# Writing a head's scaled context keys as two halves straight from their bank, with the norm's place and one step changed

## The chip, the core and the metric

The kernel runs on one core of a Trainium2 chip. The metric is the device time of one execution in microseconds (us); the lower the better. The engines are named as in the profile: PE is TensorE (PEld its weight loads), DVE is VectorE, ACT is ScalarE, POOL is GpSimd, and SP issues most transfers.

## The reference

One layer of a block over 256 latent tokens with 256 context tokens, model width 2048, batch 1, float32. Cut to what matters here:

```python
u = layer_norm(x) * (1 + scale) + shift          # and u_c from the context
p, p_c = u @ w_in, u_c @ w_in[:, :N_KV]          # one projection, split by columns
st_f = mlstm_final_state(kc, vc, *gf_c)          # context: C = sum_t w_t k_t v_t
h_f, _ = mlstm_chunked(ql, kl, vl, *gf_l, st_f)  # latent, forward and backward
h_l = h_f + flip(h_b)                            # 8 heads, keys 128, values 256
o_attn = attend_blocks(q_l, k_all, v_all)        # 16 query heads, 4 key heads
h = rms_norm(h_l per head, mh_norm_w)
y_a = (sigmoid(o_a) * h * silu(z_a)) @ w_ba
y_b = (o_attn * silu(z_b)) @ w_bb
out = (sigmoid(g_a) * y_a + sigmoid(g_b) * y_b) @ w_out
x_new = layer_norm(ALPHA * x + gate * out)
```

The change is in the eight heads of the first branch: the state `C` of a head is a product of the context's values with its keys, each key scaled by a weight `w_t` of its token and direction.

## The kernel before

**Products in three.** Every float32 operand of a product is split in two: ACT rounds it to a high half (`nc.scalar.copy`, L337) and DVE subtracts that from the original to get the low half (L338). `three` and `three_b` (L340 and on) make each product of three matmuls: high x high, high x low, low x high. So a weight block (`raw`, 128x1024, one transfer of SP) gets a cast by ACT (`whi`) and a subtraction by DVE (`wlo`) before PE can use it. Three buffers of each rotate, and `LEAD` asks for two blocks to be split ahead.

**Heads inside the gemms.** The gemms stream the weights: two for each `c` in 0 to 3, with the output gate's weights (`o`) and the silu gate's (`z`), of 32 ticks each, a tick being three matmuls of 512 columns (a triple). `head(h)` is a generator whose pieces are the steps of a head; `weave` spreads the steps over the ticks of a gemm. Head 0 lies in the `z` gemm of `c` = 0, head 1 in the next `o` gemm, and so on; head 7 lies in the first gemm of the second branch (`q`). Even heads lie in `z` gemms, odd heads in `o` gemms.

**A head's steps**, each ended by a `yield`: (1) fetch the rows of decays into `ws` through the POOL queue, transpose the context keys into a bank `pk` on PE (L849), scale them by the weights `G["wc"]` into `kw` by four ACT writes (L853), split `kw` into the halves `kwh` and `kwl` of the tile `rd`, split the context values into `rd` too; (2) split the latent keys and queries into `rc` (`kqh`, `kql`); (3) nothing; (4) and (5) the states of the two directions, `pC`, from `kwh`, `kwl` and the values, each split into `ra`; (6) `ws` becomes the decay matrix (L878 to L882, with an exponential on ACT) and the scaled queries (`rb`); (7) the scores `pS`, multiplied into `ws`; (8) `ws` split, its low half into `rc`, and the latent values into `ra`; (9) nothing; (10 to 13) four products `ph`, by tokens and direction, with a small division on DVE (L919 to L921) and the sum into `hh`; (14) the norm's root, on DVE and POOL (`rr`); (15) the norm applied to `hh`, two DVE instructions (L934); (16) transposes `pT` and their split.

**Two heads overlap.** Steps 14, 15 and 16 of a head are taken out of its list and put into the next head's list at places 1, 7 and 10:

```python
    for h in range(8):
        st = steps(head(h), HEAD_STEPS)
        if h > 0:
            for at, step in zip((1, 7, 10), order[-3:]):
                st.insert(at, step)
            order = order[:-3]
        order += st
```

**What sets the order.** The written order gives each instruction a priority; a scheduler then places instructions on the engines by its own estimate of their times. On each engine they run strictly in the order so found, and each waits for what it needs. PE's products stand as they are written; DVE and ACT are where the scheduler moves things. Banks: eight hold 512 float32 a partition each, four under the name `acc` for the gemms and four under `aux`, which `pk`, `pC`, `pS`, `pT` and `ph` take in turn.

Of the kernel before, what the change touches and what calls it, by code (L numbers as in the profile page):

```python
# [8 lines left out]
F32 = mybir.dt.float32  # L9
F32R = mybir.dt.float32r  # L10
BF16 = mybir.dt.bfloat16
AF = mybir.ActivationFunctionType
ALU = mybir.AluOpType
AX = mybir.AxisListType

P = 128
# [34 lines left out]
def block_kernel(ctx: ExitStack, tc: tile.TileContext, a: dict, out: bass.AP):  # L51
    nc = tc.nc
# [12 lines left out]
    def nm(s):  # L65
        uid[0] += 1
        return f"{s}_{uid[0]}"

    def slot(n, dt=F32):
        return big.tile([P, BIG], dt, tag="S8", name=nm(n))  # L70
# [7 lines left out]
    def t2(n):  # L78
        return tp.tile([P, 512], F32, tag="T2", name=nm(n), bufs=4)


    def sm(n, w):
        return tp.tile([P, w], F32, tag=f"sm{w}", name=nm(n), bufs=SMALL[w])
# [4 lines left out]
    def aux(n):  # L88
        return ps.tile([P, 512], F32, tag="aux", name=nm(n))
# [14 lines left out]
    def halves(x):  # L104

        return x.rearrange("p (n w) -> p w n", w=2)

    def as_halves(x):
        return x.rearrange("p (w n) -> p w n", w=2)
# [210 lines left out]
    def split_ahead(k):  # L320
        while len(ready) < k and (plan or early):
            fetch_ahead()
            raw, n = early.pop(0)
            turn[0] += 1
            pool, k_ = (late[0], 1) if late and turn[0] % 3 == 0 else (wp, 2)
            lo = pool.tile([P, 1024], F32R, tag="wlo", name=nm("wlo"), bufs=k_)[:, :n]
            hi = pool.tile([P, 1024], F32R, tag="whi", name=nm("whi"), bufs=k_)[:, :n]
            split(hi, lo, raw)
            ready.append((hi, lo))
# [5 lines left out]
    def split(hi, lo, src):  # L335

        nc.scalar.copy(hi, src)  # L337
        nc.vector.tensor_tensor(lo, src, hi.bitcast(F32), op=ALU.subtract)  # L338

    def three(o, xh, xl, wh, wl, start, stop):  # L340
        mm(o, lhsT=xh, rhs=wh, start=start, stop=False)  # L341
# [36 lines left out]
    def steps(gen, n):  # L378

        return [lambda: next(gen, None) for _ in range(n)]  # L380
# [158 lines left out]
    end, j = 0.0, 0  # L539
    for i, (c, k0, k1) in enumerate(VISITS):  # L540
        end += (k1 - k0) * (1.8 if chunks[c][1] == "w_kv" else 2.65)
        j0, j = j, max(j, min(len(units), math.ceil((end - T0) * 6 / DT)))
# [19 lines left out]
    G = {}  # L562
# [107 lines left out]
    def conv(x, hd, n, scale):  # L670

        ac = t2("cva")[:, :n * 256].rearrange("p (s t) -> p s t", s=n)
        sg = t2("cvs")[:, :n * 256].rearrange("p (s t) -> p s t", s=n)
        nc.scalar.activation(ac, x[:, :, 1:257], AF.Identity, bias=cv[:, hd, 3:4], scale=cv[:, hd, 1:2])
        nc.vector.scalar_tensor_tensor(ac, x[:, :, 0:256], cv[:, hd, 0:1], ac, op0=ALU.mult, op1=ALU.add)
        nc.vector.scalar_tensor_tensor(ac, x[:, :, 2:258], cv[:, hd, 2:3], ac, op0=ALU.mult, op1=ALU.add)
        nc.scalar.activation(sg, ac, AF.Sigmoid)
        nc.vector.scalar_tensor_tensor(x[:, :, 1:257], ac, scale, sg, op0=ALU.mult, op1=ALU.mult)
# [75 lines left out]
    j = 32  # L754
# [35 lines left out]
    gate_of = [None] * 4  # L790
# [35 lines left out]
        held.extend(lambda t=t: put_z(t) for t in range(2))  # L826
        gate_of[c] = g_

    HEAD_STEPS = 16

    def head(h):
        c, j = h // 2, h % 2
        kx = kT[h // 4][:, h % 4]
        kl = kx[:, 0, 1:257]
        q = qT[:, h, 1:257]
        stt = nc.vector.scalar_tensor_tensor
# [7 lines left out]
        kwh, kwl = (rd[:, i * 512:(i + 1) * 512] for i in range(2))  # L844
        vch, vcl = (rd[:, 1024 + i * 516:1024 + (i + 1) * 516].rearrange("p (t f) -> p t f", t=2)
                    for i in range(2))
        pk = aux("pk")
        for t in range(2):
            nc.tensor.transpose(pk[:, t * P:(t + 1) * P], kx[:, 1, 1 + t * P:1 + (t + 1) * P], ident)  # L849
        kw = t2("kw")  # L850
        for d in range(2):
            for t in range(2):
                nc.scalar.activation(kw[:, (2 * d + t) * P:(2 * d + t + 1) * P], pk[:, t * P:(t + 1) * P],  # L853
                                     AF.Identity, bias=0.0, scale=G["wc"][:, d, t, h:h + 1])
        split(kwh, kwl, kw)
        split_v(vch, vcl, va[c][:, 2:4, j, :])
        yield

        rc = wslot("rc", F32R)
        wl, kqh, kql = rc[:, 0:768], rc[:, 768:1280], rc[:, 1280:1792]  # L860
        split(kqh[:, 0:256], kql[:, 0:256], kl)
        split(as_halves(kqh[:, 256:512]), as_halves(kql[:, 256:512]), halves(q))
        yield
        yield

# [3 lines left out]
        for d in range(2):  # L869
            pc = aux("pC")  # L870
            for t in range(2):
                sl = slice((2 * d + t) * P, (2 * d + t + 1) * P)
# [17 lines left out]
        for t in range(2):  # L890
            sl = slice(t * P, (t + 1) * P)
# [8 lines left out]
        split_v(vh, vl, va[c][:, 0:2, j, :])  # L900
        yield
        yield

        hh = t2("hh").rearrange("p (t d) -> p t d", t=2)
        intra = {(0, 0): [(0, 0)], (0, 1): [(128, 0), (640, 1)],
# [2 lines left out]
        for t in range(2):  # L908
            for d in range(2):
                ph = aux("ph")  # L910
                sl = slice(d * 256 + t * P, d * 256 + (t + 1) * P)
# [18 lines left out]
        rr = sm("rr", 2)  # L930
        rsqrt(rr, ss, 1.0 / 256.0, EPS)
        yield
        for t in range(2):
            stt(hh[:, t, :], hh[:, t, :], rr[:, t:t + 1], gate_of[c][:, t, j * 256:(j + 1) * 256],  # L934
                op0=ALU.mult, op1=ALU.mult)
        yield
        pT = aux("pT")
        for f in range(2):
# [5 lines left out]
    def split_v(hi, lo, src):  # L944

        by = lambda x: x.rearrange("p t (w n) -> p t w n", w=2)
        split(by(hi), by(lo), src.rearrange("p t (n w) -> p t w n", w=2))
# [21 lines left out]
# [7 lines that stand above are left out]
    n = HEAD_STEPS  # L976
    order = [lambda h=h: conv(qT[:, h:h + 1, :], h, 1, 1.0) for h in range(8)] + order
# [183 lines left out]
    for k4 in range(4):  # L1161
        hi, lo = slot("wh", F32R), slot("wl", F32R)
        for b in range(2):
            raw = wp.tile([P, 1024], F32, tag="raw", name=nm("raw"), bufs=3)
            nc.sync.dma_start(raw, a["w_out"][3][2 * k4 + b])
            sl = slice(b * 1024, (b + 1) * 1024)
            split(hi[:, sl], lo[:, sl], raw)
        wl.append((hi, lo))
    for t in range(2):
        pp = acc("out")  # L1170
        for k in range(KT):
            sl = slice((k % 4) * 512, (k % 4 + 1) * 512)
# [99 lines left out]
```

## Time and profile before

| | |
|---|---|
| time, median of 3 runs | 1344.13 us (1340.24 to 1344.71) |
| the profiled execution | 1343.62 us, span 1341.6 us, 2.0 us around it |
| mean granted clock of PE | 0.991 |
| busy in the span | PE 97%, DVE 73%, ACT 48%, POOL 4% |
| the heads' stage | about 466 to 700 us of the span |

How to read it: PE is nearly always busy, so what a change of DVE or ACT work can give or take is the time in which PE waits for them. The wait rows name the line that waits and the line that let it go on; the rows of single instructions give their starts, so that a wait can be read as a start that comes late after the one before.

### The profile page before, as it was taken

Reading aid. Unit: us, or ns where it says so; the run is one execution under the profiler, and the core shown is the slowest. Engines: PE = TensorE matmul, PEld = TensorE weight load, DVE = VectorE, ACT = ScalarE, POOL = GpSimd, SP = SyncE. Lnnn points to the kernel's source line nnn. Section 1 sums busy time; section 2 is a strip of 40 time slices with the busy share of each in tenths; the row PEclk is TensorE's granted clock in tenths of the full one; section 3 lists DMA queues with packets and bytes.
Section 4 is the critical chain, followed back from the end, with each engine's and each line's share of the span. In section 5 each row is a group of like instructions: output and inputs, shape, how many; then the busy total and the mean of one; then the engine's idle time right before and its main releaser. Section 6 shows DMA issues by size and latency. Waiting matters only on the chain.

```text
span 1341.6 us, 19662 instructions
## 1 busy us (share of the span) xinstructions
PE 1296.4 (97%) x7541; PEld 1161.7 (87%) x7541; DVE 976.0 (73%) x1577; ACT 649.8 (48%) x928; POOL 54.1 (4%) x83
## 2 busy tenths in 40 slices
PE   6999998999999999999999999999999999999996
PEld 3788988999999988888889999998888888888884
DVE  6698998877986678787787868786555455545667
ACT  4544322324334576676755566565444444434441
POOL 0000000000110011010110000000000000000000
PEclk8999998999999999999999999999999999999999
DMA  9876764885435554555455444445655556576663
GB/s 339 310 260 227 251 221 136 296 306 189 143 111 189 195 167 160 171 181 180 155 162 182 139 161 142 143 139 174 204 198 202 204 197 203 195 275 219 218 219 116
DMA packets 77902, 264.17 MB, mean 197 GB/s; under 512 B 8984, under 2 KB 11688, under 8 KB 77168
## 3 DMA queue, kind: packets, MB, share of 16 engines
q1 hardware_dynamic: 74752, 251.99, 55.5%
q0 software_dynamic: 2448, 10.68, 2.4%
q8 instruction: 59, 0.97, 0.3%
q10 hardware_dynamic: 608, 0.24, 0.1%
q14 instruction: 35, 0.29, 0.1%
HBM read 260.75 MB, written 2.14 MB: 196 GB/s over the span
## 4 chain that ended last, share of the span: by engine, by line
PE 46%; DVE 2%; ACT 1%; DMA 1%; issue 0%; DVEq 0%; ACTq 0%
PE zb L347 2%; PE zb L346 2%; PE zb L348 2%; PE yb L343 2%; PE yb L342 2%; PE yb L341 2%; PE ga L343 2%; PE ga L341 2%; PE ga L342 2%; PE ya L343 2%; PE ya L341 2%; PE ya L342 2%; PE gb L342 2%; PE gb L343 2%; PE gb L341 2%; PE q L342 2%
## 5 line engine op out<-in xcount | busy, mean ns | idle before, releaser
L338 DVE TENSOR_TENSOR wlo<-raw,whi 128x1024 fp32r<-128x1024 f32 (+3 forms) x375 | 445.3, 1190 | 264.5 <-ACT whi L337 259.4
L337 ACT CAST whi<-raw 128x1024 fp32r<-128x1024 f32 (+3 forms) x375 | 380.2, 1016 | 449.2 <-PE p L343 130.8
L342 PE MATMUL p<-wlo,u 128*128 128x512 f32 (+1 forms) x448 | 160.1, 357 | 2.5 <-DVE wlo L338 2.4
L341 PE MATMUL p<-whi,u 128*128 128x512 f32 (+1 forms) x448 | 159.3, 358 | 2.1 <-ACT u L302 1.1
L225 DVE SCALAR_TENSOR_TENSOR junk<-mod,sc 128x1024 bf16<-128x1024 f32 x128 | 153.4, 1221 | 9.4 <-DMA mod<-in_w_mod 9.3
L343 PE MATMUL p<-whi,u 128*128 128x512 f32 (+1 forms) x448 | 159.4, 356 | 0.0
L342 PEld LDWEIGHTS p<-wlo,u 128*128 128x128 f32 x448 | 86.5, 193 | 10.8 <-DVE wlo L338 4.2
L341 PEld LDWEIGHTS p<-whi,u 128*128 128x128 f32 x448 | 85.7, 192 | 11.5 <-ACT u L302 2.5
L343 PEld LDWEIGHTS p<-whi,u 128*128 128x128 f32 x448 | 86.6, 193 | 6.8
L346 PE MATMUL zb<-u,whi 128*128 128x256 f32 x256 | 72.0, 281 | 0.0
L346 PE MATMUL p<-u,whi 128*128 128x256 f32 x256 | 70.6, 278 | 0.7 <-ACT u L302 0.7
L348 PE MATMUL p<-u,wlo 128*128 128x256 f32 x256 | 70.3, 275 | 0.2 <-DVE wlo L338 0.2
L347 PE MATMUL zb<-u,whi 128*128 128x256 f32 x256 | 70.4, 275 | 0.0
L348 PE MATMUL zb<-u,wlo 128*128 128x256 f32 x256 | 70.4, 275 | 0.0
L347 PE MATMUL p<-u,whi 128*128 128x256 f32 x256 | 70.4, 275 | 0.0
L346 PEld LDWEIGHTS p<-u,whi 128*128 128x128 f32 x256 | 48.9, 192 | 2.1 <-ACT u L302 1.2
L341 PE MATMUL z<-whi,u 128*128 128x512 f32 x128 | 49.7, 389 | 0.0
L341 PE MATMUL q<-whi,u 128*128 128x512 f32 x128 | 49.7, 388 | 0.0
L347 PEld LDWEIGHTS p<-u,whi 128*128 128x128 f32 x256 | 49.1, 192 | 0.4 <-issue 0.4
L342 PE MATMUL gb<-wlo,u 128*128 128x512 f32 x128 | 48.7, 381 | 0.8 <-DVE wlo L338 0.8
L342 PE MATMUL z<-wlo,u 128*128 128x512 f32 x128 | 49.2, 384 | 0.2 <-DVE wlo L338 0.2
L348 PEld LDWEIGHTS p<-u,wlo 128*128 128x128 f32 x256 | 49.1, 192 | 0.3 <-DVE wlo L338 0.3
(329 smaller groups left out, 3156.9 us busy)
## 6 DMA issues: line engine op xcount, KB each, us to landing
mod<-in_w_mod SPq DMA_DIRECT2D x96, 512.0 KB, 4.9
raw<-in_w_g SPq DMA_DIRECT2D x64, 512.0 KB, 4.1
raw<-in_w_o SPq DMA_DIRECT2D x32, 512.0 KB, 3.5
raw<-in_w_z SPq DMA_DIRECT2D x32, 512.0 KB, 3.6
raw<-in_w_qb SPq DMA_DIRECT2D x32, 512.0 KB, 3.6
raw<-in_w_zb SPq DMA_DIRECT2D x32, 512.0 KB, 3.4
raw<-in_w_ba SPq DMA_DIRECT2D x32, 512.0 KB, 3.5
raw<-in_w_bb SPq DMA_DIRECT2D x32, 512.0 KB, 4.1
```

Of the source, the lines that this page charges most:

```text
L225: nc.vector.scalar_tensor_tensor(junk, blk, 1.0, sc[v][:, hf * 1024:(hf + 1) * 1024], op0=ALU.mult, op1=ALU.mult, accum_out=mp[:, v, hf, j ...
L337: nc.scalar.copy(hi, src)
L338: nc.vector.tensor_tensor(lo, src, hi.bitcast(F32), op=ALU.subtract)
L341: mm(o, lhsT=xh, rhs=wh, start=start, stop=False)
L342: mm(o, lhsT=xh, rhs=wl, start=False, stop=False)
L343: mm(o, lhsT=xl, rhs=wh, start=False, stop=stop)
L346: mm(o, lhsT=wh, rhs=xh, start=start, stop=False)
L347: mm(o, lhsT=wh, rhs=xl, start=False, stop=False)
L348: mm(o, lhsT=wl, rhs=xh, start=False, stop=stop)
```

## The change

Three edits. The four scaled writes go from the bank `pk` straight into `kwh` (rounded to the high half as they are written), and each is followed by a DVE instruction that reads the same bank, multiplies by the same weight and subtracts the high half, into `kwl`; the tile `kw`, its cast and its single subtraction are gone. The two instructions that apply the norm get an order behind the low half of the next head's queries (`keys_done`). And a head has one more empty step, behind step 8, so that a gemm of 32 ticks carries 17 steps where it carried 16.

```diff
     def split(hi, lo, src):
 
         nc.scalar.copy(hi, src)
-        nc.vector.tensor_tensor(lo, src, hi.bitcast(F32), op=ALU.subtract)
+        return nc.vector.tensor_tensor(lo, src, hi.bitcast(F32), op=ALU.subtract)
...
-    HEAD_STEPS = 16
+    HEAD_STEPS = 17
+    keys_done = []
...
-        kw = t2("kw")
         for d in range(2):
             for t in range(2):
-                nc.scalar.activation(kw[:, (2 * d + t) * P:(2 * d + t + 1) * P], pk[:, t * P:(t + 1) * P],
-                                     AF.Identity, bias=0.0, scale=G["wc"][:, d, t, h:h + 1])
-        split(kwh, kwl, kw)
+                sl, wc = slice((2 * d + t) * P, (2 * d + t + 1) * P), G["wc"][:, d, t, h:h + 1]
+                src = pk[:, t * P:(t + 1) * P]
+                nc.scalar.activation(kwh[:, sl], src, AF.Identity, bias=0.0, scale=wc)
+                stt(kwl[:, sl], src, wc, kwh[:, sl].bitcast(F32), op0=ALU.mult, op1=ALU.subtract)
         split_v(vch, vcl, va[c][:, 2:4, j, :])
         yield
...
-        split(as_halves(kqh[:, 256:512]), as_halves(kql[:, 256:512]), halves(q))
+        keys_done.append(split(as_halves(kqh[:, 256:512]), as_halves(kql[:, 256:512]), halves(q)).ins)
...
         split(wh, wl, w)
         split_v(vh, vl, va[c][:, 0:2, j, :])
+        yield
         yield
         yield
...
-        for t in range(2):
-            stt(hh[:, t, :], hh[:, t, :], rr[:, t:t + 1], gate_of[c][:, t, j * 256:(j + 1) * 256],
-                op0=ALU.mult, op1=ALU.mult)
+        with tc.issue_after(keys_done[-1]):
+            for t in range(2):
+                stt(hh[:, t, :], hh[:, t, :], rr[:, t:t + 1],
+                    gate_of[c][:, t, j * 256:(j + 1) * 256], op0=ALU.mult, op1=ALU.mult)
```

The edits shift what the scheduler places around them. First DVE, from the low half of head 3's decays (`rc<-ws`) to the building of head 4's `ws`; before:

```order
L338 TENSOR_TENSOR rc_5591<-ws_5554,rb_5682 128x768
L338 TENSOR_TENSOR act_5738<-pT_5733,act_5738 128x512
L338 TENSOR_TENSOR wlo_5755<-raw_5696,whi_5756 128x1024
L919 SCALAR_TENSOR_TENSOR r_5768<-ph_5761,gT 128x1
L920 TENSOR_TENSOR r_5768<-ph_5761,r_5768 128x1
L921 RECIPROCAL r_5768<-r_5768 128x1
L338 TENSOR_TENSOR wlo_5804<-raw_5727,whi_5805 128x1024
L878 SCALAR_TENSOR_TENSOR ws_5846<-ws_5846,gT,cst 128x256
L879 SCALAR_TENSOR_TENSOR ws_5846<-ws_5846,gT,cst 128x256
L880 SCALAR_TENSOR_TENSOR ws_5846<-ws_5846,gT,cst 128x128
L919 SCALAR_TENSOR_TENSOR r_5789<-ph_5779,gT 128x1
L881 SCALAR_TENSOR_TENSOR ws_5846<-ws_5846,gT,cst 128x128
```

and in the changed kernel, whose lines stand one to three further down:

```order
L338 TENSOR_TENSOR rc_5595<-ws_5557,rb_5686 128x768
L338 TENSOR_TENSOR wlo_5759<-raw_5700,whi_5760 128x1024
L338 TENSOR_TENSOR act_5742<-pT_5737,act_5742 128x512
L879 SCALAR_TENSOR_TENSOR ws_5850<-ws_5850,gT,cst 128x256
L338 TENSOR_TENSOR wlo_5808<-raw_5731,whi_5809 128x1024
L921 SCALAR_TENSOR_TENSOR r_5775<-ph_5768,gT 128x1
L880 SCALAR_TENSOR_TENSOR ws_5850<-ws_5850,gT,cst 128x256
L922 TENSOR_TENSOR r_5775<-ph_5768,r_5775 128x1
L881 SCALAR_TENSOR_TENSOR ws_5850<-ws_5850,gT,cst 128x128
L923 RECIPROCAL r_5775<-r_5775 128x1
L882 SCALAR_TENSOR_TENSOR ws_5850<-ws_5850,gT,cst 128x128
```

The first of the four instructions on the fetched `ws` now stands ahead of a weight block's low half and of the first division, which both stood before it; the other three are mixed with the division.

Second DVE again, where head 4's context keys get their low halves (`rd<-kw` before, `rd<-pk` after) and head 3's norm is applied; before:

```order
L338 TENSOR_TENSOR rd_5848<-va_876,rd_5848 128x516
L128 TENSOR_SCALAR rs_5874<-ss_5760 128x2
L934 SCALAR_TENSOR_TENSOR hh_5759<-hh_5759,rr_5873,G_5025 128x256 x2
L338 TENSOR_TENSOR wlo_5895<-raw_5802,whi_5896 128x1024
L338 TENSOR_TENSOR rd_5848<-kw_5852,rd_5848 128x512
L338 TENSOR_TENSOR rc_5883<-kT_444,rc_5883 128x256
L338 TENSOR_TENSOR rc_5883<-qT_3947,rc_5883 128x256
```

and after:

```order
L856 SCALAR_TENSOR_TENSOR rd_5852<-pk_5853,gT,rd_5852 128x128
L923 RECIPROCAL r_5840<-r_5840 128x1
L338 TENSOR_TENSOR rc_5888<-kT_444,rc_5888 128x256
L927 SCALAR_TENSOR_TENSOR hh_5766<-ph_5833,r_5840,hh_5766 128x256
L856 SCALAR_TENSOR_TENSOR rd_5852<-pk_5853,gT,rd_5852 128x128
L338 TENSOR_TENSOR rc_5888<-qT_3947,rc_5888 128x256
L338 TENSOR_TENSOR wlo_5900<-raw_5806,whi_5901 128x1024
L856 SCALAR_TENSOR_TENSOR rd_5852<-pk_5853,gT,rd_5852 128x128
L128 TENSOR_SCALAR rs_5879<-ss_5767 128x2
L937 SCALAR_TENSOR_TENSOR hh_5766<-hh_5766,rr_5878,G_5027 128x256 x2
L856 SCALAR_TENSOR_TENSOR rd_5852<-pk_5853,gT,rd_5852 128x128
```

The norm stands behind the queries' low half (`rc<-qT`) now, but still ahead of the last of the four low halves. In odd heads the product of the silu gate (`sz`) stands at that place instead of the norm.

Third ACT, the same keys of head 4 in the changed kernel, with what each instruction waits for (an engine's name is its semaphore):

```order
L855 ACTIVATE rd_5852<-pk_5853,gT 128x128 [waits PE_49]
L337 CAST rc_5888<-kT_444 128x256
L337 CAST rc_5888<-qT_3947 128x256
L855 ACTIVATE rd_5852<-pk_5853,gT 128x128 [waits DVE_49]
L337 CAST whi_5901<-raw_5806 128x1024 [waits DMAHW4_49,PE_49,Activation_49]
L929 ACTIVATE sq_5845,ss_5767<-hh_5766 128x256 [waits DVE_49]
L855 ACTIVATE rd_5852<-pk_5853,gT 128x128 [waits DVE_49]
L812 ACT_TABLE_LOAD
L812 ACTIVATE G_5605<-o_5606 128x512 [waits PE_49]
L855 ACTIVATE rd_5852<-pk_5853,gT 128x128 [waits DVE_49]
```

Before, these four writes stood together, the second to fourth without a wait; now each waits for DVE's low half of the one before, and other work stands between them. On PE the order keeps nine triples between `pk` and the first `pC` (eight in head 7). The scores `pS` come one triple earlier, the first `ph` has nine triples behind `pS` where it had seven (seven for five in head 7), and one triple less lies between the last `ph` and the next `pk`.

## Rows read from the trace of the kernel before

**Rows 1.** The page's head and its first row: busy time, share, instructions.

```profile
span 1341.6 us, 19662 instructions
PE 1296.4 (97%) x7541; PEld 1161.7 (87%) x7541; DVE 976.0 (73%) x1577; ACT 649.8 (48%) x928; POOL 54.1 (4%) x83
```

**Rows 2.** PE's waits in 440 to 720 us: total, times, longest.

```profile
PE pC L343 <- DVE rd L338: 5.6, 5, 1.4
PE ph L343 <- DVE rc L338: 3.0, 4, 1.3
PE pC L341 <- ACT rd L337: 0.7, 1, 0.7
...
```

**Rows 3.** PE's timeline: start, duration, instruction; idle time in brackets.

```profile
484.97 0.38 PE L343 MATMUL ph<-ra,rc 128*128 128x258 f32 x1
...
580.09 0.38 PE L849 MATMUL pk<-cst,kT 128*128 128x128 f32 x2
...
586.22 0.30 PE L341 MATMUL pC<-rd 128*128 128x258 f32 x1
586.36 0.28 PE L342 MATMUL pC<-rd 128*128 128x258 f32 x1
588.05 0.38 PE L343 MATMUL pC<-rd 128*128 128x258 f32 x1 [1.42 <-DVE rd L338]
...
685.22 0.38 PE L343 MATMUL ph<-ra,rc 128*128 128x258 f32 x1 [1.32 <-DVE rc L338]
```

**Rows 4.** Stretches in head 2: busy of PE, PEld, DVE, ACT, POOL; clock; DMA.

```profile
527.00:530.00 3.00, 1.22 (x6) 0.62 (x5) 2.81 (x5) 2.98 (x5) 0.15 (x1) 0.99 0.01 3
530.00:534.00 4.00, 4.00 (x16) 3.49 (x17) 2.76 (x4) 3.99 (x7) 1.80 (x2) 0.58 0.37 131
```

**Rows 5.** DVE's timeline, from head 3's decays to head 4's keys.

```profile
571.65 0.96 DVE L338 TENSOR_TENSOR rc<-ws,rb 128x768 fp32r<-128x768 f32 x1 [0.90 <-ACT rb L337]
...
577.05 0.48 DVE L878 SCALAR_TENSOR_TENSOR ws<-ws,gT,cst 128x256 f32<-128x256 f32 x1 [1.11 <-DMA ws<-rows]
...
582.46 1.23 DVE L338 TENSOR_TENSOR wlo<-raw,whi 128x1024 fp32r<-128x1024 f32 x1 [0.45 <-ACT whi L337]
583.61 0.80 DVE L338 TENSOR_TENSOR rd<-va,rd 128x516 fp32r<-128x516 f32 x1
584.33 0.14 DVE L128 TENSOR_SCALAR rs<-ss 128x2 f32<-128x2 f32 x1
585.37 0.88 DVE L934 SCALAR_TENSOR_TENSOR hh<-hh,rr,G 128x256 f32<-128x256 f32 x2 [0.90 <-POOL rr L129]
586.17 1.22 DVE L338 TENSOR_TENSOR wlo<-raw,whi 128x1024 fp32r<-128x1024 f32 x1
587.30 0.69 DVE L338 TENSOR_TENSOR rd<-kw,rd 128x512 fp32r<-128x512 f32 x1
```

**Rows 6.** ACT's timeline in the same head.

```profile
578.60 1.28 ACT L882 ACT_TABLE_LOAD   x1 [3.23 <-DVE r L920]
...
583.51 1.12 ACT L853 ACTIVATE kw<-pk,gT 128x128 f32<-128x128 f32 x4
584.51 1.06 ACT L337 CAST whi<-raw 128x1024 fp32r<-128x1024 f32 x1
585.44 0.64 ACT L337 CAST rd<-kw 128x512 fp32r<-128x512 f32 x1
...
586.77 1.28 ACT L812 ACT_TABLE_LOAD   x1
```

**Rows 7.** The tile `ws`, all heads: min/median/max ns; its transfers to landing.

```profile
L880 DVE SCALAR_TENSOR_TENSOR ws<-ws,gT,cst x8: 344/348/357, 384.0 to 662.3; 128x128 f32<-128x128 f32 x8
...
DMA to landing us min/median/max: 3.8/4.6/5.9
```

**Rows 8.** The tile `hh`: DVE's sum, which reads the bank `ph`.

```profile
L925 DVE SCALAR_TENSOR_TENSOR hh<-ph,r,hh x16: 480/484/486, 488.3 to 693.4; 128x256 f32<-128x256 f32 x16
```

**Rows 9.** POOL's timeline: the issue of head 4's `ws`.

```profile
572.91 0.58 POOL L842 DMA_DIRECT2D ws<-rows  x1 [16.38 <-DVE rc L338]
```

## Prediction

> **What bounds the kernel now.** I read the page first: PE is busy in 97% of the span [rows 1], so nothing that DVE or ACT lose or win counts unless PE waits for it. The wait view comes next, cut to the heads' stage, the only place that the change touches. It shows 9.7 us of PE waits there: 5.6 and 0.7 in front of the states `pC`, for the low and high halves of the scaled keys, 3.0 in front of the first `ph`, for the low half of the decays [rows 2], and 0.4 in two small rows and a weight block. These rows undercount. A wait row begins only at the modelled end of the matmul before, so I read starts: products of 258 columns that follow at once start 0.11 us apart, of 512 columns 0.215 us. In head 4 the second and third product of `pC` start 1.69 us apart [rows 3], 1.58 too much, where the row says 1.42. [...]
>
> **The new place of things.** I take head 4 as the pattern and count from its transposes `pk`, at 580.09 [rows 3]. The first product of `pC` starts at +6.13 [rows 3]; without stalls the second group's last product, which needs the fourth low half, is due at 6.13 + 0.66 + 1.29 + 0.55 = +8.63 (a group of six, two triples, five more products). The nine triples between `pk` and `pC` stay.
>
> *The fetched rows.* The low half of head 3's decays ends at 572.61, POOL issues head 4's `ws` at 572.91 [rows 5, 9], and DVE stands at its first use until 577.05, -3.04 [rows 5]. Transfers took 3.8 to 5.9 us to land, median 4.6 [rows 7]. The change leaves the issue behind the same instruction, at nearly the same distance from the next `pk`: the DVE work between an odd head's keys and that low half adds up to 11 us, after which it ends 7.2 us ahead of `pk` (7.5 now). I keep -2.8, between 4.6 and the 4.14 of this head. But DVE now meets this wait ahead of a weight block and of the first division. Behind it stand 1.13 us of weight block (586.17 to 587.30 [rows 5]) and the division's three steps. ACT's table load, which followed 1.55 us behind the landing (577.05 to 578.60 [rows 5, 6]), moves to about 2.95 behind it, +0.15. The division also frees the bank that the next `pk` takes, through ACT's first part of `hh`: `pk` itself waits about 0.5 us in such a head, and the first weight block of the next gemm arrives about 0.9 late. Both are swallowed by what comes next.
>
> *The first scaled write.* From table load to scaled keys it takes 4.91 us now (578.60 to 583.51 [rows 6]); one square and its reading, 0.4, move behind, so 4.5, and the write starts at +4.7, against +3.42 now.
>
> *The four pairs.* Now the writes, the cast and the subtraction take 4.48 us from the first write (583.51 to 587.99 [rows 5, 6]). The cast of 0.64 and its subtraction of 0.69 go. In their place come four DVE instructions of 128 columns; the nearest row, the same operation and width from SBUF, is 0.35 [rows 7], and the wider one that reads a bank, 0.484 for 256 columns [rows 8], is no dearer than its like from SBUF, 0.48 [rows 5]. I take 0.35; bounds 0.27 (starts of queued neighbours) and 0.48. Laid end to end, four cost DVE 0.7 more than now and ACT 0.5 less, which idle time of both would hide. What costs is the alternation that the order shows. The second write waits for the first low half, which stands behind a weight block (1.13) and the values' low half (0.72, 583.61 to 584.33 [rows 5]); counted from the first write it comes at +1.5. Then a weight cast (0.93, 584.51 to 585.44 [rows 6]) and a square; DVE's weight block starts at +2.9 behind that cast, the third low half at +4.0. Then in an even head POOL's answer to the norm, 1.04 us (584.33 to 585.37), two norms of 0.80 together (585.37 to 586.17 [rows 5]), and only then the fourth: +6.1 to +6.45. The fourth write itself is ready at about +5.5, behind a table load of 1.28 [rows 6] and a sigmoid of 0.5. In an odd head the gate's product stands in the norm's place and the fourth ends at +6.3.
>
> [...]
>
> [...]
>
> **The sum.** Even heads 4 and 6: the fourth low half ends at 4.7 + 6.45 = +11.2 against +8.63, 2.6 late (now 1.7 and 2.1). Head 2: its transfer was among the slow ones, 3.3 (now 3.9, slow clock included; bounds 2.6 and 4.5). Odd heads 3 and 5: the even head before ends its decays 9.1 ahead of `pk`, so the rows land at about -4.4, the first write starts at +3.1, the fourth ends at +9.4: 0.85 each (now 1.2 and 1.0). Head 1 keeps the old order ahead of its table load: 0.1 (now 2.2). Head 0: nothing (0.3). Head 7 has one triple less: 1.5, and at `ph` the decays' low half ends 20.3 behind `pk` where 19.0 is asked, 1.35: together 2.85 (3.2). The waits at the `ph` of heads 0, 1, 3 and 5 go: two more triples, one of them taken by the earlier `pS`, give 0.65 us and more from one weight block less ahead of the scores' product, against 0.3 to 0.9. Total 3.3 + 2 x 2.6 + 2 x 0.85 + 0.1 + 2.85 = 13.2 us, against 15.5: 2.3 us less. From the profiled execution's 1343.6 (2.0 of it around the span), which is 0.5 below the median of the runs, that makes **1341.3 us**. SP's weight transfers move with the weight blocks' subtractions by under 2 us, and two blocks stand ready; POOL's instructions keep their order.
>
> **Rivals.** What a measurement of this kernel can tell from no change is about 0.3%, 4 us: 1339.6 to 1347.6.
>
> *Faster: the handing over is hidden.* If the rows land 0.8 us sooner (the shortest, 3.8 [rows 7]), and the late pairs hand over as quickly as ACT and DVE do elsewhere, even heads lose 1.8 or less, odd heads nothing, head 7 some 2: about 7.5 us in all, 8 less than now, 1335.6. For it: all of the old `pC` waits had their cause in one late subtraction, and half of the keys is now ready early. Against it: the fourth low half behind the norm.
>
> [...]
>
> *Nothing happens:* the norm stands behind the queries but ahead of the last low half, so the wait only changes its name; 1343.6.
>
> **How the numbers follow.** The exchange of stalls as worked out: 0.50, own range 1337 to 1346; a fifth of it lies below 1339.6. Hidden handing over: 0.23. Late rows: 0.20. Nothing: 0.07. So faster 0.10 + 0.23 = 0.33, same 0.40 + 0.07 = 0.47, slower 0.20. Both sides hold much, so the range runs from below the faster case, 1334, to the slower one's edge, 1348.5.
>
> **What would show it.** Right: the cast and `kw` gone; four short writes and four low halves, ACT waiting for DVE between them; `ph <- rc` nearly gone from PE's waits except in head 7; PE waiting at the second `pC` group of even heads for `rd`, 1 us or more; DVE idle 2 to 3 us for `ws` each head. Wrong: no idle time of DVE at `ws`, or no wait at the second group (faster); several stretches at half clock, or weight blocks late by 1 us and more (slower).

## The result, and the profile after

The changed kernel takes 1361.51 us (median of 4 runs; 1359.74 to 1361.81), the kernel before, run beside it, 1343.68 us: a ratio of 1.0132 [1.0113, 1.0150], slower by 17.8 us. The forecast was 1341.3.

The page's head and PE's row of the changed kernel, which answer to [rows 1]:

```profile
span 1359.7 us, 19686 instructions
PE 1301.6 (96%) x7541; PEld 1160.3 (85%) x7541; DVE 977.9 (72%) x1601; ACT 645.4 (47%) x920; POOL 51.8 (4%) x83
```

No engine has work that would explain 18 us: PE's busy time is 5 us up for the same 7541 instructions, DVE's 2 us up, ACT's 4 us down. So most of it is waiting. PE's waits in the heads' stage of the changed kernel (engine, line, who is waited for: total us, times, longest), to be held against [rows 2]:

```profile
PE pk L850 <- ACT hh L925: 12.0, 6, 3.1
PE pC L343 <- DVE rd L856: 4.7, 6, 1.3
PE o L342 <- DVE wlo L338: 2.1, 4, 0.8
PE z L342 <- DVE wlo L338: 1.9, 4, 0.8
PE ph L343 <- DVE rc L338: 1.1, 1, 1.1
PE q L342 <- DVE wlo L338: 0.8, 1, 0.8
```

Counted by late starts, as the prediction does for head 4's `pC` but with every start, the stage (440 to 735 us) lost 17.3 us before and loses 35.5 now. The 18.2 between them is the whole loss: the two profiled executions differ by 18.2 (1361.81 and 1343.62). The waits at `ph` are gone but for head 7, and those at `pC` are smaller than before. The new ones are the transposes `pk` of heads 2 to 7 (12.9 us by starts: 3.25, 1.24, 2.52, 1.93, 2.84, 1.12) and the first weight block behind each of them in heads 3 to 7, 1.0 us each. So the place to read is what lies ahead of `pk`. DVE's timeline there, head 3's end and head 4's beginning in the changed kernel, against [rows 5]:

```profile
574.74 0.95 DVE L338 TENSOR_TENSOR rc<-ws,rb 128x768 fp32r<-128x768 f32 x1
575.61 1.22 DVE L338 TENSOR_TENSOR wlo<-raw,whi 128x1024 fp32r<-128x1024 f32 x1
576.74 0.68 DVE L338 TENSOR_TENSOR act<-pT,act 128x512 fp32r<-128x512 f32 x1
582.71 0.48 DVE L879 SCALAR_TENSOR_TENSOR ws<-ws,gT,cst 128x256 f32<-128x256 f32 x1 [5.29 <-DMA ws<-rows]
583.11 1.22 DVE L338 TENSOR_TENSOR wlo<-raw,whi 128x1024 fp32r<-128x1024 f32 x1
584.24 0.15 DVE L921 SCALAR_TENSOR_TENSOR r<-ph,gT 128x1 f32<-128x1 f32 x1
...
585.03 0.16 DVE L923 RECIPROCAL r<-r 128x1 f32<-128x1 f32 x1
...
595.41 1.90 DVE L937 SCALAR_TENSOR_TENSOR hh<-hh,rr,G 128x256 f32<-128x256 f32 x2 [0.90 <-POOL rr L129]
597.24 0.34 DVE L856 SCALAR_TENSOR_TENSOR rd<-pk,gT,rd 128x128 fp32r<-128x128 f32 x1
```

DVE stands for 5.29 us in front of the fetched rows, with a weight block's low half and the first division behind it in its queue. The issue of that fetch on POOL, ACT's first part of `hh`, and PE, in the same head:

```profile
575.99 0.58 POOL L843 DMA_DIRECT2D ws<-rows  x1 [12.24 <-DVE rc L338]
```

```profile
585.28 0.47 ACT L925 ACTIVATE hh<-ph,r 128x256 f32<-128x256 f32 x1 [7.24 <-DVE r L923]
...
590.11 0.36 ACT L855 ACTIVATE rd<-pk,gT 128x128 fp32r<-128x128 f32 x1
```

```profile
585.81 0.44 PE L850 MATMUL pk<-cst,kT 128*128 128x128 f32 x2 [2.37 <-ACT hh L925]
...
590.56 0.48 PE L342 MATMUL z<-wlo,u 128*128 128x512 f32 x1 [0.78 <-DVE wlo L338]
...
597.63 0.38 PE L343 MATMUL pC<-rd 128*128 128x258 f32 x1 [1.34 <-DVE rd L856]
```

Read in order: rows land 6.7 us after their issue (575.99 to 582.71), the weight block's low half takes 1.13, the division ends at 585.19, ACT reads the bank at 585.28, and `pk`, which takes that bank, starts at 585.81 instead of about 583.3. Over all heads, DVE's wait for the rows and their landing, from the view of the tile `ws` (before: 11.5 us in the view of waits, and [rows 7]):

```profile
  DMA ws<-rows: 36.4, 7
...
DMA to landing us min/median/max: 4.8/6.9/7.3
```

Why do the rows land later? The transfers of these microseconds by queue (packets, MB, share of 16 engines; q0 carries the rows, q1 SP's weights), from issue to landing in head 4, first the kernel before, then the changed one:

```profile
q0 software_dynamic: 144, 0.52, 36.6%
q1 hardware_dynamic: 73, 0.28, 18.2%
...
ws<-rows POOLq DMA_DIRECT2D x1, 512.0 KB, 4.1
```

```profile
q1 hardware_dynamic: 280, 1.01, 40.8%
q0 software_dynamic: 144, 0.52, 21.2%
...
ws<-rows POOLq DMA_DIRECT2D x1, 512.0 KB, 6.6
```

The same 0.52 MB of rows has 0.28 MB of weights beside it before and 1.01 MB, two blocks, after. SP's timelines show where the second block comes from. Before, SP issued its two blocks at 574.37 and 575.97, 1.5 and 3.1 us behind the rows (572.91); in the changed kernel at 574.85 and 576.85, 1.1 ahead of the rows and 0.9 behind them (575.99). Each of these issues comes 0.02 to 0.03 us after the end of a weight block's subtraction on DVE, which gives a raw buffer back; in the changed kernel one such subtraction stands directly ahead of `rc<-ws` and one directly behind it. The first block is through by 578.0, when the rows' packets have just begun (577.8, 1.8 us behind their issue, where it was 1.3 before); the second shares the rest of the time with them. From 578.0 to 579.5 the two queues moved only 0.13 MB together, and no run shows why. That the weights make the rows late was tried (below).

### The profile page after: what moved, and what is told of

Read it like the earlier page. It is cut to its first block, busy times and chain, and to the rows that moved or that the text cites. A ratio compares the mean times of both kernels' runs of the same rounds, so it can differ in the third digit from the quotient of the medians.

```text
span 1359.7 us, 19686 instructions
## 1 busy us (share of the span) xinstructions
PE 1301.6 (96%) x7541; PEld 1160.3 (85%) x7541; DVE 977.9 (72%) x1601; ACT 645.4 (47%) x920; POOL 51.8 (4%) x83
## 4 chain that ended last, share of the span: by engine, by line
PE 72%; DVE 13%; DMA 7%; ACT 4%; issue 3%; POOL 0%; SPq 0%; DVEq 0%; ACTq 0%; POOLq 0%
PE p L342 5%; PE p L343 5%; PE p L341 5%; DVE wlo L338 4%; DMA ws<-rows 4%; PE p L346 2%; DVE junk L225 2%; PE zb L348 2%; PE zb L346 2%; PE zb L347 2%; PE p L347 2%; PE p L348 2%; PE yb L342 2%; PE yb L343 2%; PE yb L341 2%
## 5 line engine op out<-in xcount | busy, mean ns | idle before, releaser
L342 PE MATMUL o<-wlo,u 128*128 128x512 f32 x128 | 49.9, 390 | 2.2 <-DVE wlo L338 2.1
L341 PE MATMUL o<-whi,u 128*128 128x512 f32 x128 | 49.9, 390 | 0.0
L342 PE MATMUL q<-wlo,u 128*128 128x512 f32 x128 | 48.9, 382 | 0.9 <-DVE wlo L338 0.8
```

The lines of the kernel that those rows point to most:

```text
L342: mm(o, lhsT=xh, rhs=wl, start=False, stop=False)
```

## The experiments

**Theory A**: the added step lets the scheduler put the wait for the rows ahead of the first division, and two weight blocks beside the rows make that wait long. **Rival B**: the alternation of ACT and DVE over the four pairs costs. Rivals C (the late norm), D (late rows cost wherever the wait stands) and E (what else the step moves) are stated where they matter. Each kernel was timed in five rounds beside the kernel before (1343 to 1344 us).

### The parts alone

Four kernels: the one before with only the step; with only the direct halves; with only the norm's order; and the changed kernel without the step.

```diff
# e1_step_alone
-    HEAD_STEPS = 16
+    HEAD_STEPS = 17
...
         split_v(vh, vl, va[c][:, 0:2, j, :])
+        yield
         yield
```

> The kernel before with only the one more empty step. Theory A (the step sets VectorE's order: the wait for the rows of ws comes ahead of the first division of ph, and the late landing of the rows falls on pk): slower than before by 8 to 16 us, pk waits of 1 to 3 us in heads 2 to 7. Rival B (the alternation of ScalarE and VectorE in the four pairs of key halves is what costs): within 3 us of before, since the pairs are not there.

> The kernel before with only the direct halves: no added step, the norm free to go where it went. Theory A: within 4 us of before, no pk waits above 1 us. Rival B: slower by 10 us or more, waits of the pC products for the low halves of 1.5 us in every even head.

> The kernel before with only the norm's order behind the next head's keys. Theory A: within 3 us of before. Rival B: the same; a third theory, C (the late norm delays the transposes of the finished head), has 3 us or more here and waits of the PE for hh.

> The changed kernel without the added step: direct halves and the norm's order, 16 steps. Theory A: within 4 us of before, that is some 14 to 20 us under the changed kernel. Rival B: still 10 us or more above before.

| kernel | us | ratio to before | PE's late starts, 440 to 735 |
|---|---|---|---|
| step alone | 1365.18 | 1.0164 [1.0150, 1.0178] | 36.1 |
| direct halves alone | 1339.70 | 0.9979 [0.9964, 0.9993] | 14.9 |
| norm's order alone | 1343.25 | 0.9994 [0.9984, 1.0004] | 18.4 |
| changed, without the step | 1339.98 | 0.9975 [0.9960, 0.9991] | 14.8 |

The empty step is the whole loss and more (+21.5 us, over the 8 to 16 expected); the direct halves gain 3.7 to 4 us (by the intervals 1 to 5); the norm's order gives nothing. Rivals B and C fall. But theory A's `pk` waits were not found in the step alone. Its largest wait:

```profile
PE pC L341 <- ACT rd L337: 17.3, 6, 3.4
...
PE pk L849 <- ACT hh L924: 1.2, 1, 1.2
```

DVE's and ACT's timelines of that kernel in head 4 show the same wait, in the middle of the first division, and where it comes out:

```profile
584.32 0.15 DVE L920 SCALAR_TENSOR_TENSOR r<-ph,gT 128x1 f32<-128x1 f32 x1
586.63 0.49 DVE L878 SCALAR_TENSOR_TENSOR ws<-ws,gT,cst 128x256 f32<-128x256 f32 x1 [2.16 <-DMA ws<-rows]
587.03 0.15 DVE L921 TENSOR_TENSOR r<-ph,r 128x1 f32<-128x1 f32 x1
```

```profile
587.75 0.47 ACT L924 ACTIVATE hh<-ph,r 128x256 f32<-128x256 f32 x1 [4.61 <-DVE r L922]
...
596.32 1.28 ACT L812 ACT_TABLE_LOAD   x1
597.61 0.60 ACT L812 ACTIVATE G<-o 128x512 f32<-128x512 f32 x1
598.11 0.61 ACT L337 CAST rd<-kw 128x512 fp32r<-128x512 f32 x1
```

Here ACT begins `hh` late and does a gate's sigmoid with its table load, 1.8 us, ahead of the keys' high half. Whether the wait or that order costs 17.3 us, the next kernels tell.

### The wait moved, and the wait removed

The first and last of these hold DVE's five instructions on the rows behind the second division, without changing what they wait for; the middle two let all heads share one buffer for `ws`, so that the fetch need not wait for the low half of the decays (its columns are free earlier).

```diff
# e5_hold (on the changed kernel), e8_step_hold (on the step alone)
+        with tc.issue_after(divided[4 * h - 3]) if h else contextlib.nullcontext():
+            stt(w[:, 0:256], pm[:, 0:256], g1(0, 0), cap[:, 0:256], op0=ALU.add, op1=ALU.min)
...
-                nc.vector.reciprocal(r, r)
+                divided.append(nc.vector.reciprocal(r, r).ins)
...
# e6_rows_early (on the changed kernel), e7_rows_early_no_step
-        ws = wslot("ws")
+        ws_of or ws_of.append(wslot("ws"))
+        ws = ws_of[0]
```

> The changed kernel, with VectorE's five instructions on the rows of ws (the four sums, the product with the queries) held behind the reciprocal of the finished head's second ph, so that VectorE does the weight block's low half and two divisions before it can wait for the rows. The rows still land late. Theory A (the place of the wait on VectorE is what costs): the pk waits of 12.0 us fall below 3, the waits for the first weight block (4.0 us) below 2, and the time falls by 11 to 17 us, to 1344 to 1351. Rival D (rows that land 2 us later are paid wherever the wait stands): 1355 or more, the stall moved to ph, pS or pC. Rival E (the added step costs through other things that it moves, ScalarE's key halves and gates): 1355 or more with the pk waits gone.

> The changed kernel, with one buffer for ws that all heads share, so that the rows' transfer waits only for the readers of its own columns (the halves of pa) and not for the low half of w: it is issued some 4 to 5 us earlier. Theory A and rival D: VectorE's wait for the rows (36.4 us) falls under 8, pk waits fall below 3, and the time comes to 1340 to 1349. Rival E: the waits fall as well, the time stays at 1355 or more.

> The changed kernel without the added step, with the shared buffer for ws. VectorE's wait for the rows there was 9.4 us, after the first division. If this wait still delays the path (theory A): 1334 to 1338, under the 1340 without the shared buffer. If what is left is not the rows: 1338.5 to 1341.5, the same as without it.

> The kernel before with the added step alone (1365.2 us) and the five instructions on the rows held behind the second reciprocal. Theory A: 1346 to 1353, the waits of pC for ScalarE's key halves (17.3 us) down to a few us, since these were late only because the divisions were. Rival E: 1358 or more, the pC waits still above 10 us, since ScalarE does a gate's sigmoid with its table ahead of the high half of kw whatever VectorE does.

| kernel | us | ratio to before | DVE's wait for the rows | landing, median |
|---|---|---|---|---|
| changed, held | 1343.00 | 1.0000 [0.9984, 1.0017] | 13.8 | 6.3 |
| changed, rows early | 1338.28 | 0.9973 [0.9956, 0.9990] | 7.7 | 4.8 |
| no step, rows early | 1343.25 | 0.9989 [0.9971, 1.0008] | 14.2 | 5.2 |
| step alone, held | 1348.89 | 1.0041 [1.0025, 1.0057] | 12.9 | 5.8 |

Holding takes 18.5 us off the changed kernel, the whole loss and a little more than theory A expected, with rows that land nearly as late. Early rows take 23.2 off. DVE's timeline of the held kernel in head 4, where the rows took 7.2 us:

```profile
573.20 0.16 DVE L928 RECIPROCAL r<-r 128x1 f32<-128x1 f32 x1
576.06 0.48 DVE L883 SCALAR_TENSOR_TENSOR ws<-ws,gT,cst 128x256 f32<-128x256 f32 x1 [2.69 <-DMA ws<-rows]
```

and PE's waits in the stage, all of them:

```profile
PE z L342 <- DVE wlo L338: 4.2, 3, 1.4
PE ph L343 <- DVE rc L338: 1.1, 1, 1.1
PE o L342 <- DVE wlo L338: 0.4, 1, 0.4
```

DVE still waits 2.69 us, but both divisions are done, `pk` finds its bank free and the waits at `pC` are gone too. So rival D falls: with rows that land nearly as late, the place of the wait decides. (The waits for a weight block did not go below 2 as expected. Behind each of the three at `z` PE ran 3.4 us at a granted clock of 0.50, which by an estimate, half of that time, makes 5 us more in this execution.) Rival E keeps a share in the kernel without direct halves: held, the step alone still has 6.7 us at `pC` for ACT (17.3 before it was held) and stays 5 us above before. There 16.3 of the 21.5 us go with the wait, coming out through ACT. The 5 that stay are hardly waits: these add up to 11.3 us against 9.7 before. In the profiled executions PE ran 13.7 us at a clock of 0.50 with the step, held or not, and 3.4 before, by the same estimate 5 us more.

The kernel without the step and with early rows missed both of its expectations, theory A's by 5 us, and shows the same thing at another place. Its PE waits, and DVE in head 4:

```profile
PE ph L343 <- DVE rc L338: 10.0, 6, 2.4
```

```profile
596.34 0.69 DVE L887 TENSOR_TENSOR ws<-ws,qT 128x512 f32<-128x512 f32 x1 [3.09 <-DMA ws<-rows]
596.95 0.95 DVE L338 TENSOR_TENSOR rc<-ws,rb 128x768 fp32r<-128x768 f32 x1
```

With its buffer free earlier, the product on the rows was placed ahead of the low half of the decays: a wait of 3.09 us now holds up `rc`, and `ph` behind it.

### Fewer weights beside the rows

Each weight block of the output gates and the silu gates is fetched only by its first half, which is then used for both halves; the other half of these weights is left out.

```diff
# e9_half_weights (on the changed kernel; w_o and w_z only)
-            src, n = plan.pop(0)
+            src, n, *cut = plan.pop(0)
+            m = n // 2 if cut and cut[0] else n
...
-            nc.sync.dma_start(raw, src)
+            nc.sync.dma_start(raw[:, :m], src[:, :m])
+            if m < n:
+                raw = raw[:, None, :m].to_broadcast([P, 2, m])
...
-            plan.extend(b[1:] for b in row_blocks(a[w][c], 512, range(KT)))
+            plan.extend((src, n, w in ("w_o", "w_z")) for _, src, n in row_blocks(a[w][c], 512, range(KT)))
```

> The changed kernel, its order on every engine untouched, but each weight block of the output gates and z gates (the work beside the heads) is fetched only by its first half, 256 KB for 512 KB, and both halves of the split block are made from it (the other half of these weights is left out of the computation). If the rows land late because two weight blocks move beside them: landing falls from 6.9 to about 5 us (the before-run's transfers with 150 to 280 KB of weights beside them took 3.5 to 4.2 us to their last packet, the changed kernel's with 1,000 KB 6.2 to 6.9), VectorE's wait for the rows falls from 36.4 to 20 to 27 us, the pk waits from 12 to 3 to 7, and the time by 6 to 12 us, to 1349 to 1356. If the late landing has another cause (the issue itself, the queue that the rows share with the gate row): landing 6.5 or more and the time within 3 us of 1361.5.

1347.66 us, 1.0026 [1.0009, 1.0043] to before: 13.9 us under the changed kernel, with the same order on every engine. PE's wait at `pk`, and the tile `ws`:

```profile
PE pk L854 <- ACT hh L929: 1.2, 3, 0.5
```

```profile
  DMA ws<-rows: 22.4, 7
...
DMA to landing us min/median/max: 4.1/4.6/6.6
```

The maximum is a control inside the run: head 7 lies beside the `q` gemm, whose blocks were left whole. The queues from issue to landing, for head 7's rows:

```profile
q1 hardware_dynamic: 279, 1.01, 42.0%
q0 software_dynamic: 144, 0.52, 26.0%
...
ws<-rows POOLq DMA_DIRECT2D x1, 512.0 KB, 6.6
```

With 1.01 MB beside them they take 6.6 us as in the changed kernel; head 4's, with 0.51 MB, took 4.7. So the weights beside the rows make them late. The time fell further than expected: with rows 2 us earlier `pk`'s bank is free almost in time, and 2.0 of the 12.9 us by starts are left there. The first weight block still comes 1.0 us late in four heads.

### Both cures together

Shared buffer, and the rows' instructions held behind the first reciprocal (`divided[4 * h - 4]`): on the changed kernel, on it without the step, and on the kernel before.

> The changed kernel with both: the shared buffer for ws (1338.3 us alone) and the five instructions on the rows held behind the first reciprocal of the finished head, so that they can neither wait ahead of the low half of w (3.2 us of ph waits in the run with the shared buffer) nor ahead of the weight block's low half (3.3 us of z waits). If these two waits are what VectorE's early turn at the rows leaves: 1333 to 1337. If the waits only move: 1337 to 1341.

> The same two edits on the changed kernel without the added step. The shared buffer alone made this one 3 us slower there (1343.3 for 1340.0), with 10.0 us of ph waits, which theory A puts on VectorE's wait for the rows coming ahead of the low half of w (rc). Held behind the first reciprocal that wait can't come there: ph waits under 3 us and 1333 to 1338. If the ph waits have another cause they stay at 8 us or more and the time at 1342 to 1345.

> The kernel before with the shared buffer for ws and the rows' instructions held behind the first reciprocal, nothing of the change in it. If the 12 us that the run of both edits gained on the 16-step kernel are the rows' and the direct halves' shares added: the halves and the norm's order were worth 3.3 to 4 us by themselves, so 1333 to 1336 here. If the early rows are worth something only together with the direct halves: 1338 to 1343.

| kernel | us | ratio to before | PE's late starts |
|---|---|---|---|
| changed | 1343.45 | 0.9998 [0.9985, 1.0011] | 18.7 |
| changed, without the step | 1330.66 | 0.9914 [0.9895, 0.9934] | 6.6 |
| before | 1333.88 | 0.9923 [0.9901, 0.9945] | 8.0 |

All of PE's waits in the stage of the second:

```profile
PE pC L343 <- DVE rd L861: 2.5, 3, 1.3
PE ph L343 <- DVE rc L338: 0.4, 1, 0.4
```

Without the step the `ph` waits fall from 10.0 to 0.4 us, as expected, and 1330.66, below its expectation, beats both kernels: the one before beside it by 12 us, the changed one by 31. The gain comes from the rows: the kernel before gets 9 us from them alone; the 3 us between it and the best one fit the direct halves' 4, but their intervals overlap. On the changed kernel the combination missed even the weaker expectation: no wait for the rows is left, and 5.8 us of waits at `pC` (six, up to 1.7) appear, for low halves that stand behind the norm and the latent values' low half. Yet its waits, 6.5 us in all, are no more than the 6.9 of the changed kernel with early rows alone, which is 5 us faster. What differs is the clock: PE ran 13.7 us of the stage at a granted clock of 0.50 here, behind the stalls at `pC` of heads 2, 4 and 6, and none there; half of that, 7 us, is the estimate of its price. Head 4's stall and what followed (rows as in [rows 4]):

```profile
588.90:590.90 2.00, 0.36 (x1) 0.19 (x1) 2.00 (x3) 0.71 (x3) 0.77 (x1) 1.00 0.42 164
590.90:594.30 3.40, 3.18 (x9) 2.49 (x9) 2.94 (x5) 2.54 (x5) 1.30 (x1) 0.50 0.43 141
```

Why the scheduler places the low halves so with the step was not followed further, and no run holds the clock apart from the stalls.

## Why the prediction was wrong

**The fetched rows: the step that failed.** "The change leaves the issue behind the same instruction... I keep -2.8", that is a landing of 4.1 to 4.6 us. The issue did stay there, but it took 6.7 in head 4 and 6.9 in the median. The prediction moved SP's weight transfers "by under 2 us" and set that at nothing because two blocks stood ready for PE. It looked at what SP's transfers owe to PE, not at what they share with POOL's. The trace of before had the warning: head 2's transfer, which was taken as an accident of that head, landed in 5.9 us with 0.94 MB of weights beside it, head 4's in 4.1 with 0.28. In the changed kernel, from 578.0 to 582.4 us, when nearly all of head 4's rows moved, q0 moved 0.48 MB and q1 0.52: about half each.

**The place of the wait: seen, and its price cut off.** "DVE now meets this wait ahead of a weight block and of the first division... `pk` itself waits about 0.5 us in such a head, and the first weight block of the next gemm arrives about 0.9 late. Both are swallowed by what comes next." The chain was right link by link, and the weight block's 0.9 measured 1.0. Wrong were the 0.5, which was 1.1 to 3.3 with rows 2 us later, and above all "swallowed": a stall of PE at `pk` moves PE's whole later program, and nothing catches up, since the late starts add up to the whole loss. These two terms are 12.9 and some 5 us, where the sum had none. The stall at `pk` goes with the wait moved (1343.00) and nearly goes with the weights halved (1347.66); that is shown. The late weight block stays in four heads with the weights halved, 4.7 us behind `pk` as before, so it seems to hang on the order behind the division more than on the landing; no run tells these apart.

**The four pairs: right in kind, smaller.** A low half from the bank takes 0.342 us (0.35 taken). The fourth low half ended 11.8 us behind `pk` in head 4 (11.2 forecast). The stall at `pC` was 1.5 us in even heads and 0.4 in odd ones, for 2.6 and 0.85, since PE's own waits in between set its due time back. The exchange itself is a gain: 4 us, a little more than the 2.3 forecast, as the halves alone and the kernel without the step show.

**Heads 0, 1, 3 and 5 at `ph`** are free of waits, as forecast; head 7 kept 1.3 (1.35 forecast). The norm's order changes nothing measurable, as the sum had it. The 15.5 us that the sum takes for the kernel before are its starts in 466 to 700 us that come 0.1 us or more behind the 0.11 and 0.215 us of products that follow at once; in 440 to 735 us, with every start, they are the 17.3 above. For the changed kernel the sum had 13.2, and the stage lost 35.5.

**The rivals.** The chance of 0.20 for late rows had the right cause: the rows took 6.9 us to land in the median, where the forecast kept 4.1 to 4.6, and six heads stalled at `pk`. The clock is not the difference: the changed kernel has one stretch at half clock, 3.4 us at a granted 0.50 behind the 3.25 us at head 2's `pk` (the window's row, as in [rows 4]), and the kernel before has one of 3.4 us in head 2 as well:

```profile
522.50:527.00 4.50, 4.50 (x15) 3.64 (x15) 2.43 (x9) 4.49 (x9) 0.00 (x0) 0.62 0.24 88
```

It cost 1.6 us by the starts. So the slower side's edge of 1348.5 was 13 us short, and no run shows stretches at half clock that late rows add to this kernel, which were to be the sign of that side. The faster rival, 1335.6, did not come either: without its step the change stands at 1339.98, about half way to it.

## What to carry to other kernels

DVE took its queue strictly in order: in head 4 of the changed kernel a weight block's low half, whose cast ended at 578.05, started at 583.11, behind the 5.29 us for the rows. So ask of each wait what stands behind it: the same late transfer cost 18 us with two divisions behind the wait, and with them ahead of it at most the 3 us that lie between the held kernel and the one without the step. A scheduler that places by its own estimates can make that choice from one empty step; look at the order for instructions that wait for a transfer, and hold them behind what others are waiting for. When a subtraction moves, so does the buffer that it frees and the transfer that this starts, 0.02 to 0.03 us behind it in head 4: look for the small transfer that then has to share, as the rows did, 4.1 us beside 0.28 MB and 6.6 beside 1.01.

## What was not expected of the hardware

The two instructions of the norm took 1.90 us together in head 4 of the changed kernel, against 0.88 in [rows 5]. POOL's timeline of the changed kernel at that time:

```profile
595.57 1.46 POOL L813 TENSOR_TENSOR G<-G,mh 128x512 f32<-128x512 f32 x1 [0.19 <-ACT G L812]
```

POOL's product began beside the first of them, which kept 0.49 us, and lay beside the second, which took 1.50. In the kernel before, the norm lay apart from it and all 16 took 479 to 489 ns; there POOL's products lay beside subtractions of weight blocks, which took up to 2.27 us for 1.22. In the changed one the second of the norm took 1495 to 1499 ns in heads 2, 4 and 6. The fourth low half, which reads one of its inputs from a bank, kept its 0.34 us beside POOL's next product (597.26 to 598.54). Why the one took longer and the other did not, no run shows. The slower norm delayed the fourth low half by about 1 us in such a head, which no step of the prediction held.
